# Batched matmul: two batches in one input tile, contracted in two row tiles of TensorE

## Chip, cores and metric

The kernel runs on one core of a Trainium2 chip. The metric is the device time of one execution in microseconds (us); of several executions the median is given. Engines are named as in the profile: PE is the matrix engine TensorE (PEld its weight loads, PEq its sequencer), DVE is VectorE, ACT is ScalarE, POOL is GpSimd, and SP is SyncE, which issues the DMAs.

## The reference

Sixteen independent products of 512x512 float32 matrices, the first operand transposed:

```python
batch, m, k, n = 16, 512, 512, 512
a: [batch, k, m]   b: [batch, k, n]      # float32
out = np.matmul(a.transpose(0, 2, 1), b)  # [batch, m, n], float32
```

Each batch reads 1 MB (1,048,576 bytes) of `a` and 1 MB of `b`, and writes 1 MB. In all 33.55 MB are read and 16.78 MB written.

## The kernel before

One batch is the unit of work. The contraction index of 512 is laid out as 128 partitions with 4 consecutive DRAM rows each, so a partition's part of a load is one run of 8 KB. Per batch the stages are:

- **SP, `load(i)`** (L61, L62) issues one 1 MB DMA for `a` and one for `b`, into one of `NL = 5` pairs of float32 tiles. From the sixth load on it first waits on `s_acast`, a count of finished casts of `a`, until the tile is free.
- **DVE** casts `a` (L82) and then `b` (L84) to bfloat16, into one of `NB = 2` pairs of tiles. It waits for the load, and for the matmuls that read the bfloat16 tile two batches earlier (`s_mm`).
- **PE** (L96) runs 16 matmuls a batch: 4 groups of output rows (`mo`), each accumulated over 4 steps (`ko`) of 128 contraction rows. Each matmul has 128x128 weights and 512 moving columns. PSUM holds four tiles of 2 x 512 float32 a partition, two for each of two consecutive batches. `s_ev0` lets a batch's matmuls start.
- **ACT** (L111) copies each PSUM tile, 128x1024 float32, to an output tile, two copies a batch. The second one counts up `s_ev1`.
- **SP, `store(i)`** (L66) waits for `s_ev1` and issues a 1 MB DMA from one of `NO = 8` output tiles. A partition holds 4 output rows, again one run of 8 KB. At the end SP waits for all stores (L75).

SP's order is written out by hand: 6 loads, then for each batch one load that is `LAG = 6` batches ahead and one store. All DMAs go through SP's one queue, so the last seven stores (batches 9 to 15) stand behind all loads.

Of the kernel before, what the change touches and what calls it, by code (L numbers as in the profile page):

```python
# [1 line left out]

# [4 lines left out]

@with_exitstack
def kernel(
    ctx: ExitStack,  # L10
    tc: tile.TileContext,
    a: bass.AP,
    b: bass.AP,
    out: bass.AP,
):
    nc = tc.nc
    P = 128
    batch, K, M = a.shape
    _, _, N = b.shape
    KO = K // P  # L20
    MO = M // P
    f32 = mybir.dt.float32
    bf = mybir.dt.bfloat16

    a_v = a.rearrange("bat (ki ko) m -> bat ki ko m", ko=KO)
    b_v = b.rearrange("bat (ki ko) n -> bat ki ko n", ko=KO)
    out_v = out.rearrange("bat (mi mo) n -> bat mi mo n", mo=MO)

    LAG = 6
    NL = 5
    NB = 2
    NO = LAG + 2
    H = MO // 2

    pool = ctx.enter_context(tc.tile_pool(name="sb", bufs=1))
    psum = ctx.enter_context(tc.tile_pool(name="ps", bufs=1, space=bass.MemoryType.PSUM))
    a_ts = [pool.tile([P, KO, M], f32, name=f"a{j}") for j in range(NL)]
    b_ts = [pool.tile([P, KO, N], f32, name=f"b{j}") for j in range(NL)]  # L40
    abf_ts = [pool.tile([P, KO, M], bf, name=f"abf{j}") for j in range(NB)]
    bbf_ts = [pool.tile([P, KO, N], bf, name=f"bbf{j}") for j in range(NB)]
    o_ts = [pool.tile([P, MO, N], f32, name=f"o{j}") for j in range(NO)]
    ps_ts = [psum.tile([P, 2, N], f32, name=f"ps{j}") for j in range(NB * H)]

    s_a = [tc.alloc_semaphore(f"s_a{j}") for j in range(NL)]
    s_b = [tc.alloc_semaphore(f"s_b{j}") for j in range(NL)]
    s_o = [tc.alloc_semaphore(f"s_o{j}") for j in range(NO)]
    s_acast = tc.alloc_semaphore("s_acast")
    s_bcast = tc.alloc_semaphore("s_bcast")  # L50
    s_mm = tc.alloc_semaphore("s_mm")
    s_ev0 = tc.alloc_semaphore("s_ev0")
    s_ev1 = tc.alloc_semaphore("s_ev1")

    with tc.tile_critical(no_gpsimd_drain=True):  # L55
        def load(i):
            j = i % NL
            if i >= NL:

                nc.sync.wait_ge(s_acast, i - NL + 2)  # L60
            nc.sync.dma_start(a_ts[j][:], a_v[i]).then_inc(s_a[j], 16)  # L61
            nc.sync.dma_start(b_ts[j][:], b_v[i]).then_inc(s_b[j], 16)  # L62

        def store(i):
            nc.sync.wait_ge(s_ev1, i + 1)
            nc.sync.dma_start(out_v[i], o_ts[i % NO][:]).then_inc(s_o[i % NO], 16)  # L66

        for i in range(LAG):
            load(i)
        for i in range(batch):  # L70
            if i + LAG < batch:
                load(i + LAG)
            store(i)
        for j in range(NO):
            nc.sync.wait_ge(s_o[j], 16 * len(range(j, batch, NO)))  # L75

        for i in range(batch):
            n = 16 * (i // NL + 1)
            if i >= NB:
                nc.vector.wait_ge(s_mm, H * (i - NB + 1))  # L80
            nc.vector.wait_ge(s_a[i % NL], n)
            nc.vector.tensor_copy(out=abf_ts[i % NB][:], in_=a_ts[i % NL][:]).then_inc(s_acast, 1)  # L82
            nc.vector.wait_ge(s_b[i % NL], n)
            nc.vector.tensor_copy(out=bbf_ts[i % NB][:], in_=b_ts[i % NL][:]).then_inc(s_bcast, 1)  # L84

        nc.tensor.sem_inc(s_ev0, 1)
        with nc.tensor.Fori(0, batch // NB):
            for u in range(NB):
                a_m = abf_ts[u][:].rearrange("p ko (mi mo) -> p ko mo mi", mo=MO)
                nc.tensor.wait_ge(s_bcast, 1).then_inc(s_bcast, -1)  # L90


                nc.tensor.wait_ge(s_ev0, 1).then_inc(s_ev0, -1)  # L93
                for mo in range(MO):
                    for ko in range(KO):
                        mm = nc.tensor.matmul(  # L96
                            ps_ts[u * H + mo // 2][:, mo % 2, :],
                            a_m[:, ko, mo, :],
                            bbf_ts[u][:, ko, :],
                            start=(ko == 0),  # L100
                            stop=(ko == KO - 1),
                        )
                    if mo % 2:
                        mm.then_inc(s_mm, 1)

        for i in range(batch):
            if i >= NO:
                nc.scalar.wait_ge(s_o[i % NO], 16 * (i // NO))
            for h in range(H):
                nc.scalar.wait_ge(s_mm, H * i + h + 1)  # L110
                nc.scalar.copy(  # L111
                    out=o_ts[i % NO][:, 2 * h:2 * h + 2, :], in_=ps_ts[(i % NB) * H + h][:]
                ).then_inc(s_ev1 if h else s_ev0, 1)


# [1 line left out]
_INS = ['a', 'b']  # L117
_OUTS = [((16, 512, 512), 'float32')]


# [23 lines left out]
```

## Time and profile before

| what | value |
|---|---|
| median of 7 runs | 126.74 us (126.29 to 127.17) |
| the profiled execution's own time | 127.12 us |
| span of the profiled execution, first to last instruction | 125.1 us |
| DMA queue | 6912 packets, 50.33 MB, 96.8% of 16 engines' span |
| mean rate over the span | 402 GB/s |
| PE busy / DVE busy / ACT busy | 55% / 31% / 27% of the span |
| one cast, 128x2048 float32 to bfloat16 | 1227 ns |
| one PSUM copy, 128x1024 float32 | 1013 ns |
| mean granted TensorE clock | 0.866 of full speed |

The profile is of one execution. Its strip of 40 slices shows the busy tenths of each engine, the granted clock of PE and the rate of the DMA engines; the view of waits shows who waited for whom; the timeline shows the instructions in order, with the idle time in front of each in brackets. The time of an execution is longer than its span, here by 2.0 us.

### The profile page before, as it was taken

Reading aid. Unit: us, or ns where it says so; the run is one execution under the profiler, and the core shown is the slowest. Engines: PE = TensorE matmul, PEld = TensorE weight load, DVE = VectorE, ACT = ScalarE, POOL = GpSimd, SP = SyncE. Lnnn points to the kernel's source line nnn. Section 1 sums busy time; section 2 is a strip of 40 time slices with the busy share of each in tenths; the row PEclk is TensorE's granted clock in tenths of the full one; section 3 lists DMA queues with packets and bytes.
Section 4 is the critical chain, followed back from the end, with each engine's and each line's share of the span. In section 5 each row is a group of like instructions: output and inputs, shape, how many; then the busy total and the mean of one; then the engine's idle time right before and its main releaser. Section 6 shows DMA issues by size and latency. Waiting matters only on the chain. (4 is left out here: it accounts for less than half of the span.)

```text
span 125.1 us, 756 instructions
## 1 busy us (share of the span) xinstructions
PE 68.7 (55%) x256; PEld 29.5 (24%) x256; DVE 39.3 (31%) x32; ACT 33.7 (27%) x33; POOL 0.2 (0%) x4
## 2 busy tenths in 40 slices
PE   0008986595685807837089561957319783492000
PEld 0003433242242302323033220324103241230000
DVE  0164355435633061331603333061330603300000
ACT  4000552533623410415103360061400524033000
POOL 0000000000000000000000000000000000000000
PEclk9999999999999995999756999599965799869555
DMA  3999999999999999999999999999999999999981
GB/s 73 416 424 430 430 430 422 419 422 422 419 398 427 377 427 432 424 422 396 430 427 427 419 424 437 427 430 406 403 427 430 437 424 419 424 430 437 424 356 45
DMA packets 6912, 50.33 MB, mean 402 GB/s; under 512 B 768, under 2 KB 768, under 8 KB 768
## 3 DMA queue, kind: packets, MB, share of 16 engines
q1 hardware_dynamic: 6912, 50.33, 96.8%
HBM read 33.55 MB, written 16.78 MB: 402 GB/s over the span
## 5 line engine op out<-in xcount | busy, mean ns | idle before, releaser
L96 PE MATMUL ps<-bbf,abf 128*128 128x512 bf16 x256 | 68.7, 430 | 44.6 <-PEq L93 44.6
L111 ACT COPY o<-ps 128x1024 f32<-128x1024 f32 x32 | 32.4, 1013 | 79.8 <-PE ps L96 79.8
L96 PEld LDWEIGHTS ps<-bbf,abf 128*128 128x128 bf16 x256 | 29.5, 120 | 83.4 <-issue 65.8
L82 DVE CAST abf<-a 128x2048 bf16<-128x2048 f32 x16 | 19.6, 1227 | 49.5 <-DMA a<-in_a_dram 49.5
L84 DVE CAST bbf<-b 128x2048 bf16<-128x2048 f32 x16 | 19.6, 1227 | 19.0 <-DMA b<-in_b_dram 19.0
L111 ACT ACT_TABLE_LOAD x1 | 1.3, 1283 | 0.9 <-SPq L55 0.9
L128 POOL MEMSET const-bfloat16-1.0<- 128x1 bf16 x1 | 0.1, 102 | 0.0
L128 POOL MEMSET const-uint8-127<- 128x1 uint8 x1 | 0.1, 102 | 0.0
L128 POOL MEMSET const-float32-0.0<- 128x1 f32 x1 | 0.1, 99 | 0.2 <-issue 0.2
L128 POOL MEMSET const-float32-1.0<- 128x1 f32 x1 | 0.1, 98 | 0.0
## 6 DMA issues: line engine op xcount, KB each, us to landing
a<-in_a_dram SPq DMA_DIRECT2D x16, 1024.0 KB, 22.8
b<-in_b_dram SPq DMA_DIRECT2D x16, 1024.0 KB, 24.9
out_dram<-o SPq DMA_DIRECT2D x16, 1024.0 KB, 26.6
```

Of the source, the lines that this page charges most:

```text
L82: nc.vector.tensor_copy(out=abf_ts[i % NB][:], in_=a_ts[i % NL][:]).then_inc(s_acast, 1)
L84: nc.vector.tensor_copy(out=bbf_ts[i % NB][:], in_=b_ts[i % NL][:]).then_inc(s_bcast, 1)
L96: mm = nc.tensor.matmul(ps_ts[u * H + mo // 2][:, mo % 2, :], a_m[:, ko, mo, :], bbf_ts[u][:, ko, :], start=(ko == 0), stop=(ko == KO - 1),)
L111: nc.scalar.copy(out=o_ts[i % NO][:, 2 * h:2 * h + 2, :], in_=ps_ts[(i % NB) * H + h][:]).then_inc(s_ev1 if h else s_ev0, 1)
L128: nc = _bacc.Bacc("TRN2", target_bir_lowering=False, num_devices=1)
```

## The change

Two batches become the unit of work, a pair. A tile's 128 partitions are split in two halves of 64; one half belongs to the first batch of the pair, the other to the second. Within a half, each partition holds 8 consecutive DRAM rows of the contraction index, a run of 16 KB. What follows from it in the code:

- Loads are 2 MB DMAs of 128 runs of 16 KB (8 for `a`, 8 for `b`). Stores are 2 MB DMAs; the output tile holds both batches, so a partition has two runs of 8 KB. 48 DMAs become 24.
- `NL` goes from 5 to 3 tile pairs of twice the size, `NO` from 8 to 4, and `LAG` from 6 batches to 3 pairs.
- A cast covers 128x4096 elements. After the two casts of a pair, DVE writes one element (`dve_done`) and this counts `s_acast` up a second time; a load now waits until both of its tile pair's casts are done and this second count has come.
- A pair has 64 matmuls with 64 contraction rows each: 4 groups of output rows (`t`), 8 steps (`r`), and the two batches (`g`) alternating from one matmul to the next. The built program places them as tiles of 64x128 of the array, at row 0 for the first batch and at row 64 for the second. Each batch accumulates into PSUM tiles of its own.
- The four PSUM tiles belong to one pair: two halves `h` of the output rows for each of the two batches. There is no second set for the next pair; `s_ev[0]` and `s_ev[1]` let each half's matmuls start when ACT has copied that half of the pair before.
- ACT makes four copies a pair, then zeroes one element (`act_done`), and this counts `s_out` up, for which the store waits.

```diff
-    a_v = a.rearrange("bat (ki ko) m -> bat ki ko m", ko=KO)
-    b_v = b.rearrange("bat (ki ko) n -> bat ki ko n", ko=KO)
-    out_v = out.rearrange("bat (mi mo) n -> bat mi mo n", mo=MO)
-    LAG = 6
-    NL = 5
+    G = 2
+    Q = P // G
+    R = K // Q
+    pairs = batch // G
+    a_v = a.rearrange("(pair g) (q r) m -> pair (g q) r m", g=G, r=R)
+    b_v = b.rearrange("(pair g) (q r) n -> pair (g q) r n", g=G, r=R)
+    out_v = out.rearrange("(pair g) (c t) n -> pair c g t n", g=G, t=M // P)
+    LAG = 3
+    NL = 3
     NB = 2
-    NO = LAG + 2
+    NO = LAG + 1
...
-    ps_ts = [psum.tile([P, 2, N], f32, name=f"ps{j}") for j in range(NB * H)]
+    ps_ts = [[psum.tile([P, 2, N], f32, name=f"ps{g}{h}") for h in range(H)] for g in range(G)]
...
-                nc.sync.wait_ge(s_acast, i - NL + 2)
+                nc.sync.wait_ge(s_acast, 2 * (i - NL) + 2)
...
         def store(i):
-            nc.sync.wait_ge(s_ev1, i + 1)
+            nc.sync.wait_ge(s_out, i + 1)
             nc.sync.dma_start(out_v[i], o_ts[i % NO][:]).then_inc(s_o[i % NO], 16)
...
+            nc.vector.memset(dve_done[:, i:i + 1], 0.0).then_inc(s_acast, 1)
...
                 nc.tensor.wait_ge(s_bcast, 1).then_inc(s_bcast, -1)
+                for h in range(H):
+                    nc.tensor.wait_ge(s_ev[h], 1).then_inc(s_ev[h], -1)
+                    for t in (2 * h, 2 * h + 1):
+                        for r in range(R):
+                            for g in range(G):
+                                rows = slice(g * Q, (g + 1) * Q)
+                                mm = nc.tensor.matmul(
+                                    ps_ts[g][h][:, t % 2, :],
+                                    a_m[rows, r, t],
+                                    bbf_ts[u][rows, r, :],
+                                    start=(r == 0),
+                                    stop=(r == R - 1),
+                                )
+                                if t % 2 and r == R - 1:
+                                    mm.then_inc(s_mm, 1)
...
             for h in range(H):
-                nc.scalar.wait_ge(s_mm, H * i + h + 1)
-                nc.scalar.copy(
-                    out=o_ts[i % NO][:, 2 * h:2 * h + 2, :], in_=ps_ts[(i % NB) * H + h][:]
-                ).then_inc(s_ev1 if h else s_ev0, 1)
+                for g in range(G):
+                    nc.scalar.wait_ge(s_mm, G * H * i + G * h + g + 1)
+                    ev = nc.scalar.copy(
+                        out=o_ts[i % NO][:, g, 2 * h:2 * h + 2, :], in_=ps_ts[g][h][:]
+                    )
+                ev.then_inc(s_ev[h], 1)
+
+            nc.scalar.memzero(act_done[:, i:i + 1]).then_inc(s_out, 1)
```

More of the change, by code (lines that the diff above doesn't have):

```diff
@@ L19 @@
     _, _, N = b.shape
-    KO = K // P
-    MO = M // P
     f32 = mybir.dt.float32
     bf = mybir.dt.bfloat16
-    a_v = a.rearrange("bat (ki ko) m -> bat ki ko m", ko=KO)
-    b_v = b.rearrange("bat (ki ko) n -> bat ki ko n", ko=KO)
-    out_v = out.rearrange("bat (mi mo) n -> bat mi mo n", mo=MO)
-    LAG = 6
-    NL = 5
+    G = 2
[7 more added lines that the diff above has]
+    NL = 3
     NB = 2
-    NO = LAG + 2
-    H = MO // 2
+    NO = LAG + 1
+    T = M // P
+    H = T // 2
     pool = ctx.enter_context(tc.tile_pool(name="sb", bufs=1))
     psum = ctx.enter_context(tc.tile_pool(name="ps", bufs=1, space=bass.MemoryType.PSUM))
[L39 to L43, printed above, removed]
-    ps_ts = [psum.tile([P, 2, N], f32, name=f"ps{j}") for j in range(NB * H)]
+    a_ts = [pool.tile([P, R, M], f32, name=f"a{j}") for j in range(NL)]
+    b_ts = [pool.tile([P, R, N], f32, name=f"b{j}") for j in range(NL)]
+    abf_ts = [pool.tile([P, R, M], bf, name=f"abf{j}") for j in range(NB)]
+    bbf_ts = [pool.tile([P, R, N], bf, name=f"bbf{j}") for j in range(NB)]
+    o_ts = [pool.tile([P, G, T, N], f32, name=f"o{j}") for j in range(NO)]
+    dve_done = pool.tile([1, pairs], f32, name="dve_done")
+    act_done = pool.tile([1, pairs], f32, name="act_done")
+    ps_ts = [[psum.tile([P, 2, N], f32, name=f"ps{g}{h}") for h in range(H)] for g in range(G)]
     s_a = [tc.alloc_semaphore(f"s_a{j}") for j in range(NL)]
@@ L51 @@
     s_mm = tc.alloc_semaphore("s_mm")
-    s_ev0 = tc.alloc_semaphore("s_ev0")
-    s_ev1 = tc.alloc_semaphore("s_ev1")
+    s_ev = [tc.alloc_semaphore(f"s_ev{h}") for h in range(H)]
+    s_out = tc.alloc_semaphore("s_out")
     with tc.tile_critical(no_gpsimd_drain=True):
@@ L69 @@
             load(i)
-        for i in range(batch):
-            if i + LAG < batch:
+        for i in range(pairs):
+            if i + LAG < pairs:
                 load(i + LAG)
@@ L74 @@
         for j in range(NO):
-            nc.sync.wait_ge(s_o[j], 16 * len(range(j, batch, NO)))
-        for i in range(batch):
+            nc.sync.wait_ge(s_o[j], 16 * len(range(j, pairs, NO)))
+        for i in range(pairs):
             n = 16 * (i // NL + 1)
             if i >= NB:
-                nc.vector.wait_ge(s_mm, H * (i - NB + 1))
+                nc.vector.wait_ge(s_mm, G * H * (i - NB + 1))
             nc.vector.wait_ge(s_a[i % NL], n)
@@ L84 @@
             nc.vector.tensor_copy(out=bbf_ts[i % NB][:], in_=b_ts[i % NL][:]).then_inc(s_bcast, 1)
-        nc.tensor.sem_inc(s_ev0, 1)
-        with nc.tensor.Fori(0, batch // NB):
+            nc.vector.memset(dve_done[:, i:i + 1], 0.0).then_inc(s_acast, 1)
+        for h in range(H):
+            nc.tensor.sem_inc(s_ev[h], 1)
+        with nc.tensor.Fori(0, pairs // NB):
             for u in range(NB):
-                a_m = abf_ts[u][:].rearrange("p ko (mi mo) -> p ko mo mi", mo=MO)
+                a_m = abf_ts[u][:].rearrange("p r (c t) -> p r t c", t=T)
                 nc.tensor.wait_ge(s_bcast, 1).then_inc(s_bcast, -1)
[L93 to L106, printed above, removed]
+                for h in range(H):
+                    nc.tensor.wait_ge(s_ev[h], 1).then_inc(s_ev[h], -1)
[12 more added lines that the diff above has]
+                                    mm.then_inc(s_mm, 1)
+        for i in range(pairs):
             if i >= NO:
```

## The prediction

> **What bounds the kernel now.** I read the strip first, then the DMA queues, the groups, the timeline of the end and SP's waits.
>
> ```profile
> PE   0008986595685807837089561957319783492000
> ...
> PEclk9999999999999995999756999599965799869555
> DMA  3999999999999999999999999999999999999981
> GB/s 73 416 424 430 430 430 422 419 422 422 419 398 427 377 427 432 424 422 396 430 427 427 419 424 437 427 430 406 403 427 430 437 424 419 424 430 437 424 356 45
> ...
> q1 hardware_dynamic: 6912, 50.33, 96.8%
> ```
>
> The DMA row is 9 from the second slice to the 38th, in tenths: the 16 DMA engines never run dry. PE and DVE have holes everywhere. So the bytes set the time. The trace's packet records give the unit: 6144 packets of 8 KB with a median of 309 ns (16 x 8192 B / 309 ns = 424 GB/s, the rate of most slices) and 768 completion packets of 4 bytes, 7 to 14 ns, median 9. An engine carries 384 large packets: 384 x 0.309 = 118.7 us, from the first packet at 1.95 us to the last landing at 123.6. The span of 125.1 holds nothing else of size.
>
> The start doesn't bind: ten loads are queued at once. At the end it matters whether the last store is ready when the queue reaches it (timeline from 95 us: start, duration, work, idle before it):
>
> ```profile
> 104.14 1.23 DVE L82 CAST abf<-a 128x2048 bf16<-128x2048 f32 x1 [3.77 <-DMA a<-in_a_dram]
> 104.32 1.01 ACT L111 COPY o<-ps 128x1024 f32<-128x1024 f32 x1 [0.66 <-PE ps L96]
> 106.53 1.23 DVE L84 CAST bbf<-b 128x2048 bf16<-128x2048 f32 x1 [1.16 <-DMA b<-in_b_dram]
> ...
> 108.05 5.30 PE L96 MATMUL ps<-bbf,abf 128*128 128x512 bf16 x16 [3.77 <-PEq L93]
> ...
> 113.39 1.01 ACT L111 COPY o<-ps 128x1024 f32<-128x1024 f32 x1 [1.10 <-PE ps L96]
> ```
>
> The last `b` has landed at 106.53. The last store is issued at 114.4 and lands 9.2 us later, which is the shortest of the stores (the landing times of L66 are 9.2/26.6/30.3). Alone, eight packets an engine take 2.5 us and the way from issue to first packet 1.0 (0.94 to 1.95 at the start). So it stood some 5.5 us in the queue: seven stores behind the last load (7 x 8 x 0.309 = 17.3 us) cover the last batch's compute of 7.9 us. This cover is what the change touches.
>
> **Bytes and packets.** The bytes stay. Loads are two thirds of them; with runs of 16 KB an engine gets 128 load packets instead of 256, and 24 completion packets instead of 48. No row shows a 16 KB packet. Below: 2 x 309 ns, nothing gained. Above: a 4-byte packet, nearly all fixed cost, takes 9 ns at the median, so at most 128 x 9 = 1.15 us goes with the packets, and 24 x 9 = 0.2 with the completions. I exclude a loss: an engine reads the same kind of consecutive stretch of DRAM, cut less often. Nearest is the small packet; I take its shortest, 7 ns: (128 + 24) x 7 = **-1.1 us**. Ends: 0 and -1.35.
>
> **What the queue hides.** A pair moves 6.29 MB, 14.8 us at 424 GB/s. Loads land 22.8 us after their issue at the median, so whatever delays an issue by a few microseconds hides there:
>
> - Six loads of 2 MB (29.7 us of work) are queued at the start. Load 3 waits for pair 0's casts. Its `b` lands at about 13.3, where four MB had landed before (the second batch's `b` cast started at 13.30); two casts of twice 1.23 us (an estimate from L82 and L84) end at 15.8, and the queue lasts to 32. Waiting for `b`'s cast and the small DVE write (100 ns by POOL's 128x1 memsets) costs nothing. Without that cover it would be 2.5 us a pair.
> - SP is strict: load 4 stands behind store 0, which waits for pair 0's last copy, about 27; the queue then holds load 3 too, to 42. Later the queue is longer.
> - ACT waits for a free output tile from pair 4 on (at about 67 us); store 0 lands before 50.
> - Casts (4.9 us) and copies (4.05) per pair are far under 14.8. PSUM without a second set delays only PE, which has slack if the next point holds.
>
> **Matmuls.** A pair has 64 instead of 32, with half the contraction rows and the same 512 columns. No row shows 64 rows. Sixteen warm ones take 3.62 us (timeline, bursts after a short gap), 0.226 each. If the two batches' matmuls run side by side, 32 such slots take 7.24; if one after the other, 14.5. A slot also needs two weight loads, 108 ns each where the clock is full (1.73 us for 16): 216 ns, just under a slot. I exclude less than a slot for two, since each streams 512 columns. I take side by side: the built program puts them on separate rows of the array and separate PSUM tiles, and loads fit.
> PE idles about 5.7 us between pairs, so it starts at half clock: the five bursts after gaps of 3.8 to 4.5 us took 4.98 to 6.08 us, 1.4 to 2.5 over 3.62, 1.9 at the mean. A pair: 7.24 + 1.9 = **9.1 us** (8.6 to 9.7).
>
> [...]
>
> **The tail, on the path.** Behind the last load stand four stores of 16 packets an engine: 64 x 0.309 = 19.8 us of cover, 19.6 as before's own 17.1 (106.53 to 123.6) stands to 17.3. From the last `b` to the last landing: cast 2.45; to PE 0.26 (107.76 to 108.02); matmuls 9.1; two copies, since both batches finish together, 2.03; the zeroed element 0.1 (POOL memset 0.1; at most a copy's 1.0); issue to first packet 1.0; 16 packets 4.95; landing 0.2. Sum 20.1, **0.5 us exposed** (0 to 1.1; up to 2 with the dear zeroing). Before, none was.
>
> **Sum.** 127.12 - 1.1 + 0.5 = 126.5 against the profiled execution. That stands 0.38 above the median of 126.74, so **126.2** in the median.
>
> **Rivals.**
>
> 1. *16 KB packets move no faster* (0 for packets, +0.5 tail): 127.2. For: nothing shows the fixed share of a large packet. Against: 4-byte packets cost something.
> 2. *The last pair's matmuls outlast the cover* (slower). Place: the last pair, behind the last load; price: each microsecond beyond 8.6 is a microsecond of idle DMA engines; from 9.7 it eats the packets' gain and the change is slower. If a slot waits for two weight loads at the 0.15 us that one takes at half clock (rows at 93 to 98 us), a pair takes 32 x 0.30 + 1.9 = 11.5, exposed 2.9, 128.5; if the clock stays at half, 32 x 0.427 (weight loads then are 0.427 apart) = 13.7, exposed 5.1, 130.7. For: the granted clock falls to 5 in the very tail, and gaps grow. Against: earlier bursts warmed up after 3 to 5 us.
> 3. *The row tiles don't run side by side*, so the change doesn't do what it says: 14.5 us a pair, close to the 14.8, PE never idle and the bound from 16 on: 16 + 8 x 14.5 + 1.9 = 134, then copies, issue and store 8.3: lands at 142 for 123.6, some 145. Against: separate rows.
> 4. *More than I priced*: the whole 1.35 and a tail at its short end: 125.4.
>
> **Numbers.** My forecast 0.42; rival 1 0.18; rival 2 0.27; rival 3 0.08; rival 4 0.05. A measurement of this kernel tells about 0.3% (0.38 us) from no change: faster is below 126.36, slower above 127.12. Of my forecast (125.6 to 126.7 with the tail's bounds) three quarters are faster, the rest the same; rival 1 (126.7 to 127.8) is half the same, half slower; rivals 2 and 3 slower; rival 4 faster: faster 0.40, same 0.17, slower 0.43. No single case is as likely as mine, so the time is its 126.2. The range runs from 125.3 to 131.0, leaving out rival 3 and edges; the forecast's own is 125.6 to 126.7.
>
> **What would show it.** Load packets of 16 KB at 609 to 611 ns and 4096 + 384 packets: the packets' gain; at 618, rival 1. One pair's matmuls in 8.6 to 9.7 us with PE idle between: side by side; 14 us without idle: rival 3. A dip in the DMA row just ahead of the last store, with SP's L72 waiting for ACT: the tail. I would be wrong altogether if the DMA row fell below 9 in mid-span.

## The result and the profile after

The change made the kernel slower by 0.8%: 127.76 us in the median of 14 runs (127.00 to 128.45) against 126.73 for the kernel before (35 runs); ratio 1.0082, 95% interval 1.0065 to 1.0100. The forecast was 126.2, faster than before. The profiled execution (127.14 us, span 125.4) is one of the changed kernel's shorter ones, so its trace shows less of the loss than the median has.

The page after, its strip of DMA engines and its queues:

```profile
DMA  4999999999999999999999999999999999999393
GB/s 94 397 429 423 434 429 429 444 429 423 418 429 408 358 429 457 418 429 410 452 423 429 413 426 455 421 439 405 423 447 418 444 410 423 426 429 384 141 418 149
...
q1 hardware_dynamic: 4480, 50.33, 95.5%
q8 instruction: 1, 0.02, 0.1%
```

Two things are new. In the third slice from the end the DMA row falls to 3, at 141 GB/s: the queue ran dry ahead of the last store. And there is a second queue, `q8 instruction`, with a single packet of 16 KB, which the page before doesn't have.

The groups after:

```profile
L106 PE MATMUL ps<-bbf,abf 64*128 64x512 bf16 x512 | 69.3, 435 | 46.2 <-PEq L101 46.2
L106 PEld LDWEIGHTS ps<-bbf,abf 64*128 64x128 bf16 x512 | 36.1, 118 | 78.9 <-issue 64.1
L122 ACT COPY o<-ps 128x1024 f32<-128x1024 f32 x32 | 30.9, 1016 | 83.8 <-PE ps L106 83.8
L88 DVE CAST abf<-a 128x4096 bf16<-128x4096 f32 x8 | 18.4, 2294 | 47.4 <-DMA a<-in_a_dram 47.4
...
L127 ACT ACTIVATE act_done<-act_done 1x1 uint32<-1x1 uint32 x8 | 1.6, 197 | 0.0
```

PE is busy 69.3 us with twice the matmuls (68.7 us before, 430 ns a matmul): one matmul lasts as long as before, and twice as many fit into the same busy time. A burst of one pair at full clock (granted 1.00) shows it without the clock's part:

```profile
36.64 7.10 PE L106 MATMUL ps<-bbf,abf 64*128 64x512 bf16 x64 [3.55 <-PEq L101]
```

That is 0.222 us for two matmuls of 64 rows, against 0.226 for one of 128 rows before.

The end in the timeline after (start, duration, work, idle before it):

```profile
104.23 2.29 DVE L90 CAST bbf<-b 128x4096 bf16<-128x4096 f32 x1 [2.50 <-DMA b<-in_b_dram]
...
106.83 8.67 PE L106 MATMUL ps<-bbf,abf 64*128 64x512 bf16 x64 [5.70 <-PEq L101]
...
115.52 1.93 ACT L122 COPY o<-ps 128x1024 f32<-128x1024 f32 x2 [1.47 <-PE ps L106]
117.33 0.20 ACT L127 ACTIVATE act_done<-act_done 1x1 uint32<-1x1 uint32 x1
```

The last store is issued at 117.6 and lands 6.4 us later. The busy time by stretches of the changed kernel (us, busy of each engine, PE clock, share of the DMA engines, GB/s) shows the hole:

```profile
112.00:115.00 3.00, 3.00 (x32) 1.75 (x28) 0.00 (x0) 1.93 (x2) 0.00 (x0) 1.00 1.01 426
115.00:118.00 3.00, 0.50 (x6) 0.02 (x2) 0.00 (x0) 2.01 (x3) 0.00 (x0) 1.00 0.31 131
118.00:123.00 5.00, 0.00 (x0) 0.00 (x0) 0.00 (x0) 0.00 (x0) 0.00 (x0) 0.73 0.95 395
```

From 115 to 118 us only 0.31 of the DMA engines work. In the kernel before, the same stretch:

```profile
115.00:118.00 3.00, 0.00 (x0) 0.00 (x0) 0.00 (x0) 0.00 (x0) 0.00 (x0) 0.56 1.00 423
```

The share within the hole is telling. From 116 to 118 us it is 0.14: two of sixteen engines are still at older stores (the packet records have two packets under way at 116.8 and at 117.5 us, sixteen at 60) while fourteen have nothing. The trace also records sixteen completions of each DMA. I take them for one from each engine, since there are sixteen; the trace doesn't say which engine a completion is from, so "the last engine" is the last in order of time. I use the **spread** in what follows, the time from the first engine's completion to the last one's, of one DMA:

| | at 30 us | at 60 us | at 100 us | last store |
|---|---|---|---|---|
| before | 0.4 | 1.5 | 2.4 | 2.4 |
| after | 0.9 | 2.4 | 3.1 | 0.2 (all restart after the hole) |
| after, first to 14th engine only | 0.6 | 0.6 | 1.0 | 0.1 |

The cast waits for the last engine of its load: the first engine finishes the last `b` at 101.1 us, the last one at 104.2, and the cast starts at 104.23. After, fourteen engines stay within 1.0 us; one is 1.9 us or more behind the first from the load that lands at 45 us on, and a second joins it by 89 us (2.6). In these traces a lag that has come stays while the queue is full (before, 1.4 to 1.6 us from 59 to 86 us; after, 1.8 us or more from 34 us to the hole).

### The profile page after: what moved, and what is told of

It reads as the page before. It is cut to its first block, busy times and chain, and to the rows that moved or that the text cites. A ratio compares the mean times of both kernels' runs of the same rounds, so it can differ in the third digit from the quotient of the medians.

```text
span 125.4 us, 1215 instructions
## 1 busy us (share of the span) xinstructions
PE 69.3 (55%) x512; PEld 36.1 (29%) x512; DVE 36.7 (29%) x24; ACT 32.8 (26%) x41; POOL 0.2 (0%) x4
## 3 DMA queue, kind: packets, MB, share of 16 engines
q1 hardware_dynamic: 4480, 50.33, 95.5%
## 5 line engine op out<-in xcount | busy, mean ns | idle before, releaser
L106 PE MATMUL ps<-bbf,abf 64*128 64x512 bf16 x512 | 69.3, 435 | 46.2 <-PEq L101 46.2
L106 PEld LDWEIGHTS ps<-bbf,abf 64*128 64x128 bf16 x512 | 36.1, 118 | 78.9 <-issue 64.1
L122 ACT COPY o<-ps 128x1024 f32<-128x1024 f32 x32 | 30.9, 1016 | 83.8 <-PE ps L106 83.8
L88 DVE CAST abf<-a 128x4096 bf16<-128x4096 f32 x8 | 18.4, 2294 | 47.4 <-DMA a<-in_a_dram 47.4
L90 DVE CAST bbf<-b 128x4096 bf16<-128x4096 f32 x8 | 18.4, 2294 | 22.4 <-DMA b<-in_b_dram 22.4
L127 ACT ACTIVATE act_done<-act_done 1x1 uint32<-1x1 uint32 x8 | 1.6, 197 | 0.0
L92 DVE MEMSET dve_done<- 1x1 f32 x8 | 0.5, 59 | 0.0
```

What stands on the lines that cost most here:

```text
L92: nc.vector.memset(dve_done[:, i:i + 1], 0.0).then_inc(s_acast, 1)
L106: mm = nc.tensor.matmul(ps_ts[g][h][:, t % 2, :], a_m[rows, r, t], bbf_ts[u][rows, r, :], start=(r == 0), stop=(r == R - 1),)
L122: ev = nc.scalar.copy(out=o_ts[i % NO][:, g, 2 * h:2 * h + 2, :], in_=ps_ts[g][h][:])
L127: nc.scalar.memzero(act_done[:, i:i + 1]).then_inc(s_out, 1)
```

## The experiments

Theory A: the last pair's compute outlasts the four stores behind the last load. Theory B: 16 KB packets make two engines lag. Theory C, formed after the first four runs: the instruction DMA does. Theory D, at the end: fewer changes between loads and stores are what helps. Ratios are to the kernel before in the same session, with 95% intervals.

### e1: one more store behind the last load

```diff
-    LAG = 3
+    LAG = 4
...
-    NO = LAG + 1
+    NO = LAG
```

> LAG 4 instead of 3, all else as changed: the last loads are issued ahead of store 3, so five stores of 2 MB (24.7 us) stand behind the last load instead of four (19.8). Theory A (the tail: the queue runs dry ahead of the last store, and the packets' gain is real): the dry stretch goes, 125.7 to 126.2 us, below before, and the spread over runs shrinks. Theory B (two DMA engines fall about 2 us behind the others with 16 KB load packets, and it is they who end last): little is won, 126.9 to 127.3, with the two engines still last at the end.

126.78 us, ratio 1.0026 (1.0011 to 1.0041); runs from 126.25 to 127.09, a range of 0.84 instead of 1.45. Its stretch from 115 to 118 us:

```profile
115.00:118.00 3.00, 0.00 (x0) 0.00 (x0) 0.00 (x0) 0.00 (x0) 0.00 (x0) 0.50 1.01 426
```

The hole is gone and 0.7 us with it (0.56%), so the tail of A holds. But the time didn't fall below before, as A had it; it lies between the two theories' ranges. At the end 14 engines are done by 121.3 us and the last one at 123.5, which is what B expected of the end.

### e2: loads in runs of 8 KB

```diff
-            nc.sync.dma_start(a_ts[j][:], a_v[i]).then_inc(s_a[j], 16)
+            for v in (slice(0, R // 2), slice(R // 2, R)):
+                nc.sync.dma_start(a_ts[j][:, v, :], a_v[i][:, v, :]).then_inc(s_a[j], 16)
...
-            n = 16 * (i // NL + 1)
+            n = 32 * (i // NL + 1)
```

> Each load is cut into two DMAs of 1 MB with runs of 8 KB; stores, matmuls and waits as changed. Theory A: load packets take 309 ns again, 128 x 7 ns and 16 completions more an engine, so the last load lands 1.0 us later and the time is 128.7. Theory B: the two engines no longer lag, the last load lands no later or sooner, 127.0 to 127.8.

127.69 us, ratio 1.0102 (1.0067 to 1.0137), against 1.0082. A's 128.7 is out. The time lies in B's range, but not for B's reason, since the lag stayed. Undoing the long runs cost nothing that can be told, and the spread was the same, 2.5 us at 100 us, with 14 engines within 0.6. So B falls: the lagging engine is there with 8 KB runs too. So does the -1.1 us, as far as this run can tell. (The edit also makes the load DMAs half as large; what follows on the runs' length holds for both together.)

### e3 and e4: 2 us more ahead of the last store

```diff
...
+                    if i == pairs - 1 and h and g:
+                        for x in range(2):
+                            nc.scalar.copy(out=junk[:, 2 * x:2 * x + 2, :], in_=ps_ts[g][h][:])
                     ev = nc.scalar.copy(
```

e4 has the same two copies in the kernel before, ahead of the last batch's second copy.

> The changed kernel with two more ACT copies (to an unused tile) in front of the last pair's last copy: the last store is issued 1.9 us later. Theory A: all of it is seen, 129.7. Theory B: 129.4, as the slow engines have about 0.3 us of cover left. If the tail is not on the path: 127.8.

> The kernel before with the same two extra copies ahead of the last batch's last copy: the last store is issued 2.0 us later. Both theories: hidden behind the stores that are queued, 126.7. If the tail of before was also exposed: 128.7.

e3: 129.61 us, ratio 1.0266 (1.0235 to 1.0297), 1.8% over the changed kernel, 2.3 us for a delay of 1.9: within the intervals, all of it is seen. Its stretches:

```profile
114.00:118.00 4.00, 1.42 (x14) 0.59 (x10) 0.00 (x0) 2.56 (x3) 0.00 (x0) 1.00 0.46 193
118.00:120.00 2.00, 0.00 (x0) 0.00 (x0) 0.00 (x0) 1.26 (x3) 0.00 (x0) 1.00 0.00 0
```

For two microseconds no DMA engine moves a byte. e4: 126.41 us, ratio 1.0000 (0.9985 to 1.0016): in the kernel before the same delay lies wholly behind queued stores. The tail is on the path after, and wasn't before.

### e6: the kernel before with a long PE loop

Of the traces so far, every kernel with the changed PE loop had the instruction DMA (29.6 us in after, 31.9 in e1, 30.7 in e2, 30.3 in e3, 1.07 us long), and the engines' spread rose by 0.7 to 1.2 us with the load that was then in flight (0.93 to 1.80 in after, 0.62 to 1.86 in e2). A turn of PE's loop has 32 matmuls in before and 128 after, with as many weight loads.

```diff
-        with nc.tensor.Fori(0, batch // NB):
-            for u in range(NB):
+        with nc.tensor.Fori(0, batch // (4 * NB)):
+            for u in [*range(NB)] * 4:
```

> The kernel before with PE's loop body written out for eight batches instead of two (128 matmuls a turn, as many as the changed kernel's; the same matmuls in the same order). Theory C: the traces of the changed kernel and of its variants show one 16 KB DMA on the instruction queue at 29.6 to 31.9 us that takes 1.07 us of one DMA engine; that engine then ends every load 1.2 us after the others, and the trace of before has no such DMA. By C the same DMA appears here, one engine falls about 1.2 us behind, and the time is 127.2 to 127.8. By the rival (the lag comes from 16 KB runs or from 2 MB DMAs) nothing changes, 126.5.

126.92 us, ratio 1.0036 (1.0014 to 1.0059). The queues of its page:

```profile
q1 hardware_dynamic: 6912, 50.33, 96.3%
q8 instruction: 1, 0.02, 0.0%
```

The DMA comes, at 43.6 us, and the last engine falls from 0.95 us behind the first (in the DMA that lands at 43.6) to 2.44 (in the next one, at 47.6), where it stays to the end (2.5). The mechanism is C's, without any other part of the change. The price is 0.45 us, less than the 0.7 to 1.3 that I expected. Likely part of the lag is lost in the spread that the kernel before has of its own (2.4 us at the last store); that isn't shown.

### e8, e9, e10: one pair of bfloat16 tiles, so that PE's loop is short

```diff
-    NB = 2
+    NB = 1
```

e9 is this alone, e8 has e1's edit too, and e10 e1's and e2's.

> The changed kernel with LAG 4 (five stores behind the last load, as in e1) and NB 1: one pair of bfloat16 tiles instead of two, so that PE's loop body is one pair, 64 matmuls. DVE's cast of a pair then waits for the matmuls of the pair before. Theory C: no instruction DMA, the last engine is 1.2 us earlier than in e1: 125.4 to 125.9, faster than before. If the lag comes from the 16 KB runs or the 2 MB DMAs, 126.8 as e1, or more for the later casts.

> The same with LAG 3, as changed, so with four stores behind the last load. Theory C with A: the last load lands about 1.2 us sooner, the last pair's cast waits about 0.5 us for the pair before: 126.8 to 127.2, and still a dry stretch ahead of the last store. If the fetch is not the cause: 127.8 to 128.3.

> e8 with each load cut into two 1 MB DMAs of 8 KB runs. With neither a fetch nor a dry queue in the way, the packets' gain must show here: 1.0 us more than e8 (126.4 to 126.9). If the runs' length is worth nothing, as e8.

132.49, 132.44 and 132.64 us (ratios 1.0453, 1.0498, 1.0462): all three expectations missed, since I had made a new bound. The timeline of e8:

```profile
94.15 2.29 DVE L88 CAST abf<-a 128x4096 bf16<-128x4096 f32 x1 [9.12 <-PE ps L106]
96.36 2.29 DVE L90 CAST bbf<-b 128x4096 bf16<-128x4096 f32 x1
...
107.77 2.29 DVE L88 CAST abf<-a 128x4096 bf16<-128x4096 f32 x1 [9.12 <-PE ps L106]
```

Casts and matmuls of a pair now follow each other, 13.6 us a pair (94.15 to 107.77), all through the kernel, and the last store is late by that chain. As a test of time these three tell nothing. For C their traces do: no instruction DMA in any, and the last engine is 0.0 to 0.3 us behind the 14th at 60 us, instead of 1.6 to 2.0.

### e11 and e12: PE's loop at another place in its program

Both on e1; `head_slot`, which places the loop's head in PE's program, is 0 (e11) or 238 (e12).

```diff
...
-        with nc.tensor.Fori(0, pairs // NB):
+        PE = nc.tensor.engine
+        with nc.Fori(0, pairs // NB, engines=OrderedEngineSet([PE]), head_slot={PE: 0}):
```

> [...] Theory C (one instruction DMA in the loaded queue costs one DMA engine 1.2 us, and that engine ends last): if PE is made to fetch at the start, ahead of the loads, the lag goes and the time is 125.2 to 125.9. If the DMA still comes at about 30 us, 126.8 as e1.

> [...]

126.57 us (1.0014, 1.0000 to 1.0029) and 126.89 (1.0032, 1.0020 to 1.0044), e1 again, and neither is in the 125.2 to 125.9 of C. The DMA moved with the loop (e12: 20.7 us, e11: two, at 6.0 and 34.3), which ties it to PE's program, but it never came before the loads, and the spread rose at that moment (in e12 from 0.84 to 2.02 us, with the second of e11 by 0.2).

### e13: PE warmed before each pair

```diff
...
+                nc.tensor.wait_ge(s_w, 1).then_inc(s_w, -1)
+                for x in range(11):
+                    nc.tensor.matmul(ps_ts[0][0][:, x % 2, :], warm[:, 0:P], warm[:], start=True, stop=True)
                 nc.tensor.wait_ge(s_bcast, 1).then_inc(s_bcast, -1)
...
```

> The changed kernel (LAG 3) with eleven extra matmuls on a constant tile in each pair, between the casts of a and b, so that TensorE is at full clock when the pair's own matmuls start (their sums are overwritten). Theory A: the last pair takes 7.1 to 8.0 us instead of 8.5 to 10, the last store is issued 1.0 to 1.5 us sooner, 126.4 to 126.9, and the spread over runs shrinks to that of before. If the last pair's matmuls are not on the path: 127.8.

126.99 us, ratio 1.0043 (1.0027 to 1.0059), runs from 126.61 to 127.14. Time and range over runs fell as A says, the time to just above A's 126.4 to 126.9. The trace doesn't show how: five of the eight pairs took 7.10 us (two in after), but the last one still took 8.67, after 2.4 us of idle, with a granted clock of 0.51 in its first 3.3 us. So the last pair's length is likely what varies between runs of the changed kernel (it took 8.6 to 9.6 us in the traces of after, e18, e1, e2 and e3), but this run doesn't show it.

### e14: e1 and e2 together

> e1 (LAG 4) with each load cut into two 1 MB DMAs of 8 KB runs. The queue doesn't run dry here, so what packets cost must show: 1.0 us over e1, 127.6 to 127.9. If the runs' length is worth nothing: 126.8.

126.61 us, ratio 1.0017 (1.0002 to 1.0033), e1 within the intervals. With the queue never dry, 16 KB runs are again worth nothing.

### e15 to e18: PE's program made short

```diff
...
-        with nc.tensor.Fori(0, pairs // NB):
-            for u in range(NB):
-                a_m = abf_ts[u][:].rearrange("p r (c t) -> p r t c", t=T)
+        nc.tensor.wait_ge(s_w, 1)
+        with nc.tensor.Fori(0, pairs):
+            for u in range(1):
+                a_m = ac[:].rearrange("p r (c t) -> p r t c", t=T)
...
-                                    bbf_ts[u][rows, r, :],
+                                    ac[rows, r, :],
```

e16 adds e1's edit, e17 e1's and e2's; e18 is the changed kernel unedited.

> The changed kernel (LAG 3) with PE's loop written for one pair, 64 matmuls a turn. To make that possible without changing a wait, the matmuls read a constant tile, not the cast inputs: the products are left out, the number of matmuls, their shapes and all waits stay. Theory C: no instruction DMA, no engine 1.2 us behind, the last load lands about 1 us sooner: 126.6 to 127.1. If program size is not the cause: 127.8.

> The same (matmuls on a constant tile, loop of one pair) with LAG 4, so that the queue doesn't run dry ahead of the last store. Theory C: all that the change cost is undone and the packets' gain is left: 125.2 to 125.8, clearly below before. If the lag has another cause: 126.8 as e1.

> e16 with each load cut into two 1 MB DMAs of 8 KB runs: what the longer runs alone are worth when nothing else is in the way. If 7 ns a packet, 1.0 us more than e16: 126.2 to 126.8. If the runs' length is worth nothing, as e16.

> The changed kernel itself beside these, for the same chip and hour: 127.2 to 128.0, and a second trace of it. Theory C expects the instruction DMA at about 30 us and one engine some 2 us behind again; if the first trace was a chance, neither.

| | us | ratio (95%) | instruction DMA | spread at 100 us |
|---|---|---|---|---|
| e18, changed | 127.57 | 1.0100 (1.0069 to 1.0132) | at 29.6 us | 3.0 |
| e15, short PE program | 126.86 | 1.0043 (1.0025 to 1.0061) | none | 2.3 |
| e16, and five stores behind | 126.07 | 0.9966 (0.9950 to 0.9982) | none | 2.0 |
| e17, and 8 KB runs | 125.70 | 0.9938 (0.9922 to 0.9954) | none | 1.3 |

Each row takes one thing away from the row above it. The instruction DMA is 0.57%, 0.7 us; with five stores behind the last load it is about the same (e1 against e16, 0.60%). e15 to e17 also read one constant tile in place of the two cast ones; e6, where no operand changes, shows the same DMA and a smaller price, 0.45 us. The tail is 0.77%, 1.0 us (0.56% by e1). And with both out of the way, 16 KB runs don't gain 1.0 us: they cost 0.28%, 0.35 us, so e17 did better than both of its expectations. e16 did better than before but fell short of its 125.2 to 125.8. The queues of e16 and of e17, in this order:

```profile
q1 hardware_dynamic: 4480, 50.33, 96.1%
q1 hardware_dynamic: 6784, 50.33, 97.3%
```

In e16 the packets take 96.1% of 124.3 us, 119.5 us an engine; in e17 97.3% of 123.9, 120.6.

### e19 and e20: what made e17 faster than before?

e17 has stores of 2 MB and half as many changes between loads and stores. e20 has the kernel before with SP's order in twos; e19 has 2 MB stores as well.

```diff
-    out_v = out.rearrange("bat (mi mo) n -> bat mi mo n", mo=MO)
+    out_v = out.rearrange("(pair g) (mi mo) n -> pair mi g mo n", g=2, mo=MO)
...
-        for i in range(batch):
-            if i + LAG < batch:
-                load(i + LAG)
+        for i in range(batch // 2):
+            for x in (2 * i, 2 * i + 1):
+                if x + LAG < batch:
+                    load(x + LAG)
             store(i)
...
```

> The kernel before (1 MB loads with 8 KB runs, 128-row matmuls, its short PE loop) with 2 MB stores: two batches share an output tile, and SP issues the loads of two batches, then one store. Theory D: what was worth having in the changed kernel is neither the run length nor the row tiles, but that the queue changes from loads to stores half as often, so that the DMA engines stay closer together: 125.5 to 125.9, faster than both kernels, with the last engine at most 1.5 us behind the first (before: 2.4). The last batch's compute (about 8 us) lies behind four stores of 2 MB, so the tail is covered. If 2 MB stores are worth nothing: 126.4.

> The kernel before with its 1 MB stores, only SP's order changed: loads of two batches, then two stores. Theory D: as e19, 125.5 to 126.0, since the changes between loads and stores are as few. If the size of the store DMA is what counts: 126.4.

e19: 125.80 us, ratio 0.9951 (0.9930 to 0.9972), **faster than both kernels**, with a spread of 0.7 us at 100 us and 0.8 at the last store. e20: 126.72 us, ratio 1.0025 (1.0006 to 1.0043), spread 2.0. So D's reason was wrong: the order alone gains nothing, and in this order the 2 MB store is what keeps the engines together. The strip of e19 is as even as its end is sharp:

```profile
DMA  2999999999999999999999999999999999999992
GB/s 48 424 426 426 432 424 421 424 418 421 424 421 424 400 432 429 429 426 424 429 403 429 416 421 426 434 426 424 426 424 426 424 421 426 432 424 426 429 432 101
```

Whether that is the DMA's size, or that a partition's two runs of a store now lie 1 MB apart, wasn't tried.

## Why the prediction was wrong

**The step that failed** is "I take its shortest, 7 ns: (128 + 24) x 7 = -1.1 us", together with the exclusion "I exclude a loss". The packets behaved as forecast: in the packet records 16 KB takes 611 ns at the median, 7 less than 2 x 309, and an engine's packets take 1.1 us less in e16 than in e17. What was wrong is that this is time. The end is set by the last of sixteen engines, not by the median one. In e16 the eighth engine finished the last store at 120.95 us, in e17 at 121.47: there is half of the gain. The sixteenth finished at 122.87 and 122.50. With the longer packets the spread was larger, and in place of -1.1 they are worth +0.35 us (e16 against e17), or nothing (e2, e14). The signs that the prediction named for itself all came: 4096 + 384 packets, those of 16 KB at 611 ns, a last pair of 8.67 us with PE idle before it, a dip just ahead of the last store while SP waits for ACT:

```profile
SPq L72 <- ACT act_done L127: 84.4, 8, 15.5
```

They came with a slower kernel, since none of them looks at the last engine or at PE's program.

**What the prediction left out** is PE's program. I counted the matmuls' time and not their instructions. A turn of the loop, written out for two pairs, has 128 matmuls instead of 32, and in every trace with that loop an instruction DMA comes while the load queue is full: one packet of 16,384 bytes on the queue `q8 instruction`, at 29.6 us in after. It takes 1.07 us, the last engine falls from 0.93 to 1.80 us behind the first in the load then under way and stays behind up to the hole: +0.7 us (e15 against e18), and +0.45 in e6, apart from the rest of the change. Here, where the DMA queue is busy for 95.5% of the span, a single such packet shows in the time.

**The tail** was right in kind, and its 0.5 us (0 to 1.1) was on the small side: 0.7 (e1) to 1.0 (e16 against e15). Its terms held: casts 2.29 each for 2.45, matmuls 8.67 for 9.1, copies 1.93 for 2.03, zeroing 0.20 for 0.1. What differed is the cover. I took it from the lagging engines of before; after, the first engine had finished the stores ahead at 115.7 us and fourteen of them by 116.7, while the last load had to wait for the two that lagged. Lag delays the compute, and the cover runs out by the others' clock.

**Rivals.** Rival 2 (the last pair outlasts the cover) has the place right, and its price of a microsecond for a microsecond is what e3 shows (1.9 us more, 2.3 seen); but the traces have no pair on the path longer than 9.2 us, so it was the cover that was shorter. Rival 1 was right that the packets gain no time, though they did move faster; that its 126.7 to 127.8 holds the measured time is luck, since it has neither the instruction DMA nor the stores' size. Rival 3 is out: 64 matmuls took 7.10 us at full clock (36.64 us, granted clock 1.00), 0.222 for two, against 0.226 for one of 128 rows before: here two tiles of 64 rows run side by side, and no loss is seen. What was hidden at the start and in mid-span stayed hidden; the DMA row has 9 up to the hole. One sum of the prediction doesn't come out: by its own shares its chances add up to 0.365 for faster, 0.195 for same and 0.44 for slower, not 0.40, 0.17 and 0.43; slower was the likeliest even so.

**The sum as measured**, in us against before: 2 MB stores -0.6 (e19), longer runs +0.35, instruction DMA +0.7, tail +0.7 to +1.0; together +1.15 to +1.45, for +1.0 (0.82%) and +1.25 (e18, 1.00%). I had costed the stores' size at nothing too; it was the one part of the change that gained. The last three terms are steps of one chain (e18, e15, e16, e17), so they add up to its whole by construction; what is independent is that e19's -0.6 comes close to the -0.74 that is left in e17. Nor do tail and lag simply add: in the trace of after the last engine ends the stores ahead only at 118.9 us, when the last store's first packets were due anyway (issued at 117.6, and 1.0 us from issue to first packet at the start), so by this estimate taking away the hole alone would have gained little in that execution. The slower executions of the changed kernel have no trace.

**What stays open**: why longer load packets and smaller stores spread the engines, what the second engine lost between 50 and 89 us in the trace of after, where no instruction DMA came, and what in PE's program sets the moment of the instruction DMA (6.0 to 43.6 us in the traces that have one).

## What to carry to other kernels

When the DMA queue is the bound, follow the slowest of its engines, not the mean: a single instruction DMA was seen at the end (0.45 us in e6, 0.7 in e15 against e18), and a wait for a whole load was a wait for its slowest share (the last `b` in after: 101.1 us for the first engine, 104.2 for the last, cast at 104.23). Count instructions as well as time when a loop is lengthened, as PE's was here from 32 matmuls a turn to 128, and look for an instruction queue in the DMA section of the page. When the unit of work doubles, check that the last unit's compute still fits behind the stores that are queued behind the last load; here one more store in that place (e1) won back over half of the loss.

## What the hardware showed that was not expected

- A 16 KB instruction DMA of 0.93 to 1.10 us came in each of the traces with the long PE loop (twice in e11) and in none with a short one. Where it came in mid-span the spread rose by 0.7 to 1.5 us with the load in flight (e11's second one by 0.2), and it did not go back to what it had been.
- At 100 us the engines of the full queue were 1.9 to 2.4 us apart with 1 MB stores (before, e4, e20) and 0.7 with 2 MB stores (e19), at the same packet size and with the same loads. With 2 MB stores and 16 KB load packets it was 2.0 to 2.3 (e15, e16).
- A 16 KB packet took 611 ns at the median (after) and an 8 KB one 309 (before, after), and no time was won by it.
